# Attention turns of a hybrid encoder block: a new order of scores, transposes and weighted sums on TensorE, and transposed banks read out by two engines

## The chip, the cores and the metric

The kernel runs on one core of a Trainium2 chip. The metric is the time of one execution on the device in microseconds (us); less is better. The core has a matrix engine (TensorE, "PE" in the profile, with its weight loads shown apart as "PEld"), a vector engine (VectorE, "DVE"), a scalar engine (ScalarE, "ACT"), a general one (GpSimd, "POOL") and a queue that issues transfers (SyncE, "SP"). Each has its own queue of instructions; they wait for each other through semaphores. TensorE writes into PSUM tiles of 128 x 512 float32, called banks here, of which the kernel has eight; VectorE and ScalarE read them out.

## The reference

One layer of an encoder block over 1024 tokens of width 1024. Half of the mixed width is a convolution branch, the other half is attention with 8 heads of 64, in which each query sees an 8 x 16 neighbourhood of a grid of 16 rows by 64 columns. Cut to what the change touches:

```
s = einsum("bqhd,brqchd->bhqrc", q_r, k_win) * scale     # scores in the window
s = s + bias                                             # learned, by 2-D offset
p = softmax(s, axis=(-2, -1))
out = einsum("bhqrc,brqchd->bqhd", p, v_win)
mix = concatenate([conv_out, attn_out])
x = x + mix @ w_out
x = x + (silu(h @ w_gate) * (h @ w_up)) @ w_down         # h: RMS norm of x
```

## The kernel before

The order is written out by hand (`manual_schedule`): every engine does its instructions in the order of the Python code. Up to about 228 us come the input projections and the convolution taps, from 288 us on the output projection and the feed-forward part. Between them lies the attention loop.

The attention is cut into 32 units, numbered i. A unit is one pair of heads for a block of 128 queries. Four units in a row (a "slot", `i // 4`) share a block and so a width: `WIN` and `AR` give 253, 276, 264, 288, 341, 372, 341 and 372 keys in a window, in the order of `order`. What is outside the neighbourhood carries a bias of -1e30 from tables `tab`, which are fetched by transfers from memory. The steps of a unit:

- `score_mm(i)`: TensorE, the scores of both heads (8 matmul instructions for two units), into PSUM. Units with an odd number write into two banks of the ring `mm` (4 banks), even ones into the double bank `cv`, of which there is only one.
- `score_max(i, hh)`: VectorE adds the bias, writes the negated sum into the tile `e` and keeps its extreme in `mx`. This frees the bank.
- `score_exp(i, hh)`: ScalarE takes the exponential in place and sums it. `both` is max and exp of both heads.
- `score_norm(i)`: VectorE takes the reciprocal of the sums (`rs`), GpSimd multiplies `e` by it.
- `flip(i)`: TensorE, 12 transposes in most slots; the tile `p` lies in two `mm` banks for odd i and in `cv` for even i.
- `flip_out(i)`: reads the transposed banks back into `e`. Odd units: ScalarE, one copy for each bank. Even units: VectorE, one copy of both banks.
- `weigh(i)`: TensorE, the weighted sums of the values, 12 matmuls for three groups of keys. The value rows of a window, `vw`, come by transfers (`load_window`, `load_vw`); those of one column window (two slots) are asked for two slots ahead.
- `evac_hi`, `evac_lo`: once in four units, ScalarE and VectorE turn a finished output bank into two parts.

The loop `for i in range(4, 32, 2)` takes two units in a turn, 14 turns. In a turn TensorE does the scores of i and i + 1, the transposes of i - 3 (odd) and i - 2 (even), and the weighted sums of i - 5 and i - 4. In the turns from 14 on a job of `take_parts` (a quarter of a weight: a cast on ScalarE, a subtraction on GpSimd) is done at the end of eight turns. Behind the loop (`fill(0, 4, 5)`) come projection matmuls, the transposes of units 29, 30 and 31, and the last weighted sums.

Since even scores and even transposes share the one `cv`, its users follow each other: scores of i, two max on VectorE, transposes of i - 2, their copy, scores of i + 2.

Of the kernel before, what the change touches and what calls it, by code (L numbers as in the profile page):

```python
# [71 lines left out]
def build(ctx, tc, a):  # L72
    nc = tc.nc
    pe, act, dve, pool = nc.tensor, nc.scalar, nc.vector, nc.gpsimd
# [8 lines left out]
    def G(name, dt=F32):  # L83
        return T("G", [P, 1024], 21, name, dt)
# [10 lines left out]
    def SM(name, n=8):  # L95
        return T("sm", [P, 8], 12, name)[:, :n]

    def mm(name):
        return ps.tile([P, 512], F32, tag="mm", bufs=4, name=name)

    def tp(name):
        return ps.tile([P, 512], F32, tag="tp", bufs=2, name=name)

    def cv(name):
        return ps.tile([P, 1024], F32, tag="cv", bufs=1, name=name)
# [15 lines left out]
    def lr(w):  # L121
        return w[:, :512], w[:, 512:]
# [43 lines left out]
    def take_parts(jobs, n=4, sub=pool):  # L166
        i = pos[1]
        hi, lo = chunks[i][2]()
        w = 1024 // n
        if i == 0:  # L170
            dve.tensor_copy(hi[:, :w], raws[i][:, :w])

        def part(o):
            sl = slice(o, o + w)
            split(hi[:, sl], lo[:, sl], raws[i][:, sl], (sub,), i + o > 0)
            if o + w == 1024:
                raws.pop(i)
                issue()
        pos[1] += 1
        jobs.extend(lambda o=o: part(o) for o in range(0, 1024, w))  # L180
# [183 lines left out]
    def sum_split(h):  # L364
        if h == 0:
            cr.extend([G("crh", F32R), G("crl", F32R), ST("onesr", F32R)[:, :P]])
            dve.tensor_scalar(cr[2], ident, 0.0, 1.0, op0=OP.mult, op1=OP.add)
        split(*[w[:, h * 512:(h + 1) * 512] for w in cr[:2] + cs])
# [292 lines left out]
    def table(rh, ty):  # L661
        n = AR[rh] * NCOL[ty]
        src = tf[rh, ty].rearrange("j i h c -> (j i) (h c)")
        if rh == 0 and ty == 0:
            parts = [(G(f"tab{k}")[:, :4 * n], 4 * k) for k in range(2)]
        else:
            parts = [(H(f"tab{rh}{ty}")[:, :NH * n], 0)]
        heads = []
        for w, h0 in parts:
            nc.sync.dma_start(w, src[:, h0 * n:h0 * n + w.shape[-1]])  # L670
            heads += [w[:, o:o + n] for o in range(0, w.shape[-1], n)]
        return heads
# [10 lines left out]
    def whole(n):  # L683
        return -(-n // 32) * 32
# [29 lines left out]
    tab, et, es, pTs, os_, sums, pp, mx, cvs = {}, {}, {}, {}, {}, {}, {}, {}, {}  # L714
    at = []

    def width(s_):
        rh, cb = order[s_]
        return AR[rh] * WIN[cb][1]

    def groups(s_):
        n, m = width(s_), P if s_ == 0 else 4 * WIN[order[s_][1]][1]
        return [slice(o, min(o + m, n)) for o in range(0, n, m)]

    def score_mm(i):
        s_, hp = divmod(i, 4)
        rh, cb = order[s_]
        t = rh * 4 + cb
        c0, ncol = WIN[cb]
        s2 = cv(f"s{i}") if i > 0 and i % 2 == 0 else None  # L730
        out = []
        for hh in range(2):
            s = (mm(f"s{i}{hh}") if s2 is None else lr(s2)[hh])[:, :width(s_)]
            pe.matmul(s, qT[hh * HD:(hh + 1) * HD, hp, t * P:(t + 1) * P],  # L734
                      k4[hh * HD:(hh + 1) * HD, hp, rh * 4:rh * 4 + AR[rh], c0:c0 + ncol], start=True, stop=True)
            out.append(s)
        return out

    def score_max(i, hh, s):
        s_, hp = divmod(i, 4)  # L740
        rh, cb = order[s_]
        if i not in es:
            et[i] = G(f"e{i}").rearrange("p (h n) -> p h n", h=2)
            n, gs = width(s_), groups(s_)
            es[i] = et[i][:, :, :n]
            end = gs[-1].start + whole(gs[0].stop)
            if n < end:
                pool.memset(et[i][:, :, n:end], 0.0)
            sums[i] = SM(f"rs{i}", 2)
        mx[i, hh] = SM(f"mx{i}{hh}", 1)  # L750
        dve.tensor_tensor_reduce(out=es[i][:, hh], in0=s[hh], in1=tab[rh, cb][2 * hp + hh], scale=-1.0,  # L751
                                 scalar=3.0e38, op0=OP.add, op1=OP.min, accum_out=mx[i, hh])

    def score_exp(i, hh):
        e = es[i][:, hh]
        act.activation(e, e, AF.Exp, bias=mx.pop((i, hh)), scale=-1.0, accum_out=sums[i][:, hh:hh + 1])  # L756

    def both(i, s):
        for hh in range(2):
            score_max(i, hh, s)  # L760
            score_exp(i, hh)

    def score_norm(i):
        rs = sums.pop(i)
        dve.reciprocal(rs, rs)  # L765
        for hh in range(2):
            pool.tensor_scalar(es[i][:, hh], es[i][:, hh], rs[:, hh:hh + 1], 1.0, op0=OP.mult, op1=OP.mult)  # L767


    def flip(i):  # L770
        if i % 2 == 0:
            cvs[i] = cv(f"p{i}")
        pp[i] = lr(cvs[i]) if i % 2 == 0 else [mm(f"p{i}{r}") for r in range(2)]
        gs = groups(i // 4)
        m = whole(gs[0].stop)
        for hh in range(2):
            for g, k in enumerate(gs):
                for r, pt in enumerate(pp[i]):
                    q, o = slice(r * 64, r * 64 + 64), (hh * len(gs) + g) * 64
                    pe.transpose(pt[:m, o:o + 64], et[i][q, hh, k.start:k.start + m], ident[q, q])  # L780

    def flip_out(i, r=None):
        gs = groups(i // 4)
        m, n = whole(gs[0].stop), len(gs) * P
        w = et[i].rearrange("p h n -> p (h n)")[:m, :2 * n].rearrange("p (r n) -> p r n", r=2)
        v = w.rearrange("p r (h g q) -> p r h g q", h=2, q=64)
        pTs[i] = [v[:, :, h] for h in range(2)]
        if r is None:
            dve.tensor_copy(w, cvs[i].rearrange("p (r n) -> p r n", r=2)[:m, :, :n])
        else:  # L790
            act.copy(w[:, r], pp[i][r][:m, :n])

    def weigh(i):
        s_, hp = divmod(i, 4)
        rh, cb = order[s_]
        if hp == 0:
            os_[s_] = tp(f"o{s_}").rearrange("p (c q) -> p c q", c=4)
        gs = groups(s_)
        for g, k in enumerate(gs):
            n = whole(k.stop - k.start)  # L800
            v = vwt["first"][:, g, :] if s_ == 0 else vw[cb, rh + g]
            for hh in range(2):
                c = (2 * hp + hh) * HD
                pe.matmul(os_[s_][hh * HD:(hh + 1) * HD, hp], v[:n, c:c + HD], pTs[i][hh][:n, :, g],
                          start=g == 0, stop=g == len(gs) - 1)
# [9 lines left out]
    def evac_hi(s_):  # L815
        if not at:
            at.extend(half(f"at{h}") for h in range(2))
        act.copy(at_of(s_)[0], os_[s_])

    def evac_lo(s_):  # L820
        hi, lo = at_of(s_)
        dve.tensor_tensor(lo, os_[s_], hi.bitcast(F32), OP.subtract)
# [7 lines left out]
    def load_window(cb):  # L830
        load_vw(cb, 0, 1)
        load_vw(cb, 2, 3)
# [118 lines left out]
    def fill(m, *ks):  # L951
        if not acc:
            act.activation(warm, eps, AF.Sqrt)
        if (m, 0) not in acc:
            acc[m, 0] = mm(f"pj{m}0")
        proj(m, 0, ks, OUTER)

    for i in range(4, 32, 2):
        if i == 4:
            tab[0, 1] = tab[0, 2] = table(0, 1)  # L960
        if i == 8:
            tab[1, 1] = tab[1, 2] = table(1, 1)
        if i in (8, 12):
            load_window(i // 6)
        if i in (14, 22):
            take_parts(jobs)
        sa, sc = score_mm(i), score_mm(i + 1)
        score_max(i, 0, sa)
        score_max(i, 1, sa)
        if i > 4:  # L970
            flip(i - 3)
        score_exp(i, 0)
        score_max(i + 1, 0, sc)
        score_max(i + 1, 1, sc)
        score_norm(i - 1)
        score_exp(i, 1)
        flip_out(i - 3, 0)
        flip(i - 2)
        score_exp(i + 1, 0)
        flip_out(i - 2)  # L980
        flip_out(i - 3, 1)
        score_exp(i + 1, 1)
        score_norm(i)
        if i > 4:
            weigh(i - 5)
        weigh(i - 4)
        if i % 4 == 0 and i > 4:
            evac_hi(i // 4 - 2)
        if i % 4 == 2 and i > 6:
            evac_lo(i // 4 - 2)  # L990
        if jobs:
            jobs.pop(0)()
    fill(0, 4, 5)
    score_norm(31)
    sum_split(0)
    flip(29)
    flip_out(29, 0)
# [595 lines left out]
    for half in range(2):  # L1593
# [4 lines left out]
        w = quarter(om["u"], 0, 3)[:, part_]  # L1598
# [17 lines left out]
```

## Time and profile before

| what | us |
|---|---|
| median of 3 runs | 1014.8 (1014.24 to 1015.0) |
| the profiled execution | 1014.45 |
| its span in the trace | 1012.5 |
| the attention loop in it, first scores of i = 4 to the first projection matmul behind it | 235.16 to 288.47 |

All lines of the profile are from that one execution; their times count from the start of the span. In a line of the timeline stand: start, length, engine, line of the code, operation, written tile <- read tiles, shapes, count of merged instructions, and in brackets the idle time of the engine before it with what ended it. `PE` lengths of merged matmuls contain the modelled end of the last one.

### The profile page before, as it was taken

The page shows a single profiled execution, that of the slowest core. Times are in us where ns is not written, and L with a number is a line of the kernel's source. Part 1 is how long each engine was busy: PE and PEld are TensorE (multiplying, and loading weights), DVE is VectorE, ACT ScalarE, POOL GpSimd, SP SyncE. Part 2 cuts the span into 40 slices and gives each one's busy share as a digit, 9 for nine tenths or more (in the row PEclk, how much of TensorE's full clock was granted, in tenths as well). Part 3 has the DMA queues.
Part 4 walks back from the last instruction along what each step waited for, and adds up shares of the span by engine and source line. Part 5 has one row for each costly group of instructions (what it writes and reads, how often), then busy time and mean ns, then how long its engine had stood idle before and what let it go on. Part 6 is the DMA issues. An engine that isn't in the chain of part 4 may idle for free.

```text
span 1012.5 us, 15451 instructions
## 1 busy us (share of the span) xinstructions
PE 1004.6 (99%) x5442; PEld 843.0 (83%) x5442; DVE 781.1 (77%) x1228; ACT 476.6 (47%) x1042; POOL 457.2 (45%) x385
## 2 busy tenths in 40 slices
PE   9999999999999999999999999999999999999998
PEld 8888888886788888888888888888888888888887
DVE  5788997896779376987878778778777766768874
ACT  7556357837987255432442333333433453443432
POOL 1036674535763375275656566666565200003300
PEclk9999999999999999999999999999999999999999
DMA  9416783236514520224344343433431796634631
GB/s 349 174 50 222 204 234 94 97 104 201 177 62 165 198 98 21 67 101 166 116 147 134 125 146 126 139 132 125 155 121 59 273 373 217 209 104 142 208 118 42
DMA packets 75757, 151.72 MB, mean 150 GB/s; under 512 B 14472, under 2 KB 23560, under 8 KB 75040
## 3 DMA queue, kind: packets, MB, share of 16 engines
q1 hardware_dynamic: 73664, 147.20, 43.8%
q10 hardware_dynamic: 2016, 3.54, 1.0%
q8 instruction: 43, 0.70, 0.3%
q14 instruction: 34, 0.28, 0.1%
HBM read 112.07 MB, written 44.11 MB: 154 GB/s over the span
## 4 chain that ended last, share of the span: by engine, by line
PE 93%; DVE 3%; DMA 1%; issue 1%; POOL 1%; ACT 0%; SPq 0%; DVEq 0%; POOLq 0%
PE B L118 6%; PE B L117 6%; PE B L119 6%; PE D L117 4%; PE D L118 4%; PE D L119 4%; PE z L119 3%; PE z L117 3%; PE z L118 3%; PE pj L117 3%; PE pj L119 3%; PE gl L117 3%; PE pj L118 3%; PE gl L119 3%; PE gl L118 3%; DVE cv L381 3%
## 5 line engine op out<-in xcount | busy, mean ns | idle before, releaser
L381 DVE SCALAR_TENSOR_TENSOR cv<-u,par,cv 128x1009 f32<-128x1009 f32 (+14 forms) x92 | 117.5, 1277 | 2.3
L1559 POOL TENSOR_TENSOR ou<-ou,resm 128x512 f32<-128x512 f32 x8 | 12.8, 1615 | 137.6 <-DVE ou L1550 125.7
L408 POOL TENSOR_TENSOR pa<-pa,pr 128x1022 f32<-128x1022 f32 (+5 forms) x24 | 57.9, 2414 | 37.7 <-ACT pr L407 33.7
L109 ACT CAST op<-sr 128x512 fp32r<-128x512 f32 x77 | 47.7, 619 | 56.2 <-PE B2d L119 26.4
L113 DVE TENSOR_TENSOR op<-sr,op 128x512 fp32r<-128x512 f32 x77 | 58.2, 756 | 16.6 <-ACT op L109 16.5
L109 ACT CAST op<-wd 128x512 fp32r<-128x512 f32 x54 | 33.5, 620 | 30.7 <-DVE wd L1454 19.2
L756 ACT ACTIVATE e<-e,mx 128x341 f32<-128x341 f32 (+5 forms) x64 | 35.3, 553 | 14.7 <-DVE mx L751 14.4
L1107 DVE TENSOR_TENSOR ts<-gu,ts 128x512 f32<-128x512 f32 x36 | 40.5, 1125 | 0.6
L767 POOL TENSOR_SCALAR e<-e,rs 128x341 f32<-128x341 f32 (+5 forms) x64 | 32.7, 528 | 18.1 <-DVE rs L765 17.8
L113 DVE TENSOR_TENSOR op<-wd,op 128x512 fp32r<-128x512 f32 x54 | 39.3, 727 | 1.9 <-ACT op L109 0.8
L751 DVE CUSTOM_DVE_ANT_0 e<-s,tab 128x341 f32<-128x341 f32 (+5 forms) x64 | 27.2, 481 | 13.2 <-PE s L734 11.1
L1368 DVE TENSOR_TENSOR g<-D,g 128x512 f32<-128x512 f32 x22 | 15.2, 690 | 22.7 <-PE D L119 22.7
L435 ACT ACTIVATE sq<-z,r 128x64 f32<-128x64 f32 x96 | 28.3, 330 | 4.8 <-PE z L119 4.8
L1345 ACT ACTIVATE D<-D 128x512 f32<-128x512 f32 x22 | 12.8, 582 | 35.5 <-DVE D L1344 35.5
L407 ACT ACTIVATE pr<-u,par 128x1022 f32<-128x1022 f32 (+5 forms) x24 | 27.0, 1138 | 1.6 <-ACT vs L465 1.6
L117 PE MATMUL B2d<-op 128*128 128x512 f32 x66 | 25.7, 389 | 0.0
L118 PE MATMUL B2d<-op 128*128 128x512 f32 x66 | 25.7, 389 | 0.0
L119 PE MATMUL B2d<-op 128*128 128x512 f32 x66 | 25.7, 389 | 0.0
L1061 POOL TENSOR_TENSOR sq<-sq,sq 128x512 f32<-128x512 f32 x12 | 17.6, 1466 | 16.8 <-ACT sq L1057 16.5
L780 PEld LDWEIGHTS p<-ident,e 64*128 64x128 f32 (+1 forms) x368 | 14.7, 132 | 9.2 <-issue 4.6
L1057 ACT ACTIVATE sq<-xT 128x512 f32<-128x512 f32 x16 | 10.0, 632 | 25.4 <-DVE xT L948 25.3
L435 ACT ACTIVATION_READ_ACCUMULATOR sq<-z,r 128x1 f32 x96 | 21.7, 226 | 0.0
(1493 smaller groups left out, 3756.4 us busy)
## 6 DMA issues: line engine op xcount, KB each, us to landing
gu<-in_gu SPq DMA_DIRECT2D x44, 512.0 KB
sr<-sd SPq DMA_DIRECT2D x77, 256.0 KB
sd<-sd SPq DMA_DIRECT2D x22, 512.0 KB
wd<-in_wd SPq DMA_DIRECT2D x36, 256.0 KB
sd<-g SPq DMA_DIRECT2D x33, 256.0 KB
x<-in_x SPq DMA_DIRECT2D x8, 512.0 KB
xT<-in_xp SPq DMA_DIRECT2D x8, 512.0 KB
xd<-xT SPq DMA_DIRECT2D x16, 256.0 KB
```

The lines of the kernel that those rows point to most:

```text
L109: act.copy(hi, src)
L113: eng.tensor_tensor(*[w[..., sl] for w in (lo, src, hi.bitcast(F32))], OP.subtract)
L117: pe.matmul(acc, lh, rh, start=start, stop=False, skip_group_check=True)
L118: pe.matmul(acc, lh, rl, start=False, stop=False, skip_group_check=True)
L119: pe.matmul(acc, ll, rh, start=False, stop=stop, skip_group_check=True)
L381: dve.scalar_tensor_tensor(acc[:, o], uc[:, i], dwk[:, c, t:t + 1], acc[:, o], OP.mult, OP.add)
L408: pool.tensor_tensor(pa[:, o], pa[:, o], pr[:, o], OP.add)
L435: act.activation(sq[:, h * HD:(h + 1) * HD], z[:, h * HD:(h + 1) * HD], AF.Square, scale=r, accum_out=ss[:, h:h + 1])
L751: dve.tensor_tensor_reduce(out=es[i][:, hh], in0=s[hh], in1=tab[rh, cb][2 * hp + hh], scale=-1.0, scalar=3.0e38, op0=OP.add, op1=OP.min, a ...
L756: act.activation(e, e, AF.Exp, bias=mx.pop((i, hh)), scale=-1.0, accum_out=sums[i][:, hh:hh + 1])
L767: pool.tensor_scalar(es[i][:, hh], es[i][:, hh], rs[:, hh:hh + 1], 1.0, op0=OP.mult, op1=OP.mult)
L1107: (pool if (i, n) in ON_POOL else dve).tensor_tensor(o, l, r, OP.subtract)
```

## The change

The order within a turn becomes: scores of i + 1 (odd), transposes of i - 3 (odd), scores of i (even), weighted sums of i - 5 and i - 4, transposes of i - 2 (even). VectorE and ScalarE do max and exp of the odd unit first, then of the even one. Each `flip_out`, odd or even, is done as one copy on ScalarE and one on VectorE, a bank each. `score_norm` of the odd unit is done in the same turn and no longer in the next; that of the even unit stands at the end of the turn, behind the copies of the even transposes. The first turn does `score_norm(3)` in the place of transposes, and `score_norm(31)` behind the loop is gone, as it is in the loop now.

```
-    def flip_out(i, r=None):
+    def flip_out(i, r=None, eng=None):
...
         if r is None:
             dve.tensor_copy(w, cvs[i].rearrange("p (r n) -> p r n", r=2)[:m, :, :n])
         else:
-            act.copy(w[:, r], pp[i][r][:m, :n])
+            (eng.tensor_copy if eng else act.copy)(w[:, r], pp[i][r][:m, :n])
...
-        sa, sc = score_mm(i), score_mm(i + 1)
-        score_max(i, 0, sa)
-        score_max(i, 1, sa)
-        if i > 4:
+        sc = score_mm(i + 1)
+        if i == 4:
+            score_norm(3)
+        else:
             flip(i - 3)
-        score_exp(i, 0)
-        score_max(i + 1, 0, sc)
-        score_max(i + 1, 1, sc)
-        score_norm(i - 1)
-        score_exp(i, 1)
+        sa = score_mm(i)
         flip_out(i - 3, 0)
-        flip(i - 2)
-        score_exp(i + 1, 0)
-        flip_out(i - 2)
-        flip_out(i - 3, 1)
-        score_exp(i + 1, 1)
-        score_norm(i)
+        both(i + 1, sc)
+        both(i, sa)
+        flip_out(i - 3, 1, dve)
+        score_norm(i + 1)
         if i > 4:
             weigh(i - 5)
         weigh(i - 4)
+        flip(i - 2)
+        flip_out(i - 2, 0)
+        flip_out(i - 2, 1, dve)
+        score_norm(i)
...
     fill(0, 4, 5)
-    score_norm(31)
     sum_split(0)
```

## The prediction

> **What bounds the kernel now.** I read the page first, for the engine that is never idle, then the waits of the loop, the timeline of one steady turn, the three stretches of the loop, and the timeline just behind it. The page:
>
> ```profile
> span 1012.5 us, 15451 instructions
> PE 1004.6 (99%) x5442; PEld 843.0 (83%) x5442; DVE 781.1 (77%) x1228; ACT 476.6 (47%) x1042; POOL 457.2 (45%) x385
> ```
>
> TensorE is the bound of the whole, so the change is worth what it takes from TensorE's way through the loop, as long as what follows does not give it back. The waits between 231 and 288 us (who waited, for whom, total, times, longest):
>
> ```profile
> PEld p L780 <- issue: 4.6, 15, 1.0
> PE p L780 <- DVE mx L751: 3.0, 12, 0.5
> ...
> PEld s L734 <- DVE e L789: 0.5, 2, 0.3
> ```
>
> Nearly all that TensorE waits for in the loop is ahead of transposes (L780), on the max of VectorE (L751). For the copy of the even transposes (L789) it waits only twice, 0.5 us in all. The timeline of the turn of i = 26:
>
> ```profile
> 276.33 0.88 PEld L734 LDWEIGHTS s<-kT,qT 64*128 64x128 f32 x8 [0.17 <-issue]
> 276.33 1.42 PE L734 MATMUL s<-kT,qT 64*128 64x341 f32 x8
> ...
> 276.87 0.57 ACT L818 CAST at<-o 128x512 fp32r<-128x512 f32 x1
> 277.22 0.51 DVE L751 CUSTOM_DVE_ANT_0 e<-s,tab 128x341 f32<-128x341 f32 x1 [1.15 <-PE s L734]
> 277.30 0.68 PEld L780 LDWEIGHTS p<-ident,e 64*128 64x128 f32 x12
> 277.33 0.41 ACT L109 CAST wo06h<-wo06r 128x256 fp32r<-128x256 f32 x1
> 277.58 0.53 PE L780 MATMUL p<-ident,e 64*128 64x64 f32 x12
> ...
> 277.66 0.51 DVE L751 CUSTOM_DVE_ANT_0 e<-s,tab 128x341 f32<-128x341 f32 x1
> ...
> 278.09 0.51 DVE L751 CUSTOM_DVE_ANT_0 e<-s,tab 128x341 f32<-128x341 f32 x1
> 278.29 0.48 PEld L780 LDWEIGHTS p<-ident,e 64*128 64x128 f32 x12 [0.32 <-issue]
> ...
> 278.32 0.58 PE L780 MATMUL p<-ident,e 64*128 64x64 f32 x12 [0.21 <-DVE mx L751]
> ...
> 278.84 1.53 PE L804 MATMUL o<-e,vw 128*64 128x128 f32 x24
> ...
> 278.98 0.46 ACT L791 COPY e<-p 128x384 f32<-128x384 f32 x1
> 279.04 0.94 DVE L789 COPY e<-p 128x768 f32<-128x768 f32 x1
> ...
> 279.34 0.58 ACT L756 ACTIVATE e<-e,mx 128x341 f32<-128x341 f32 x1
> ...
> 279.96 0.67 DVE L822 TENSOR_TENSOR at<-o,at 128x512 fp32r<-128x512 f32 x1
> ...
> 280.30 0.93 PEld L734 LDWEIGHTS s<-kT,qT 64*128 64x128 f32 x8 [0.17 <-issue]
> ```
>
> By steps from start to start: scores of both units 276.33 to 277.58, 1.25. Odd transposes 0.31 (0.53 less the 0.22 of the last one, a median in the row of transposes (L780) further down). Then nothing until 278.32: 0.43, in which the even transposes stand before the shared double bank until the second max (277.66) has read it. Even transposes up to the weighted sums 0.52. Weighted sums up to the next scores 1.46. Sum 3.97, the length of the turn.
>
> **The change part by part, TensorE.** The order moves the even transposes behind the weighted sums, so that 1.46 us of other work lie over the max that they wait for. The price of each part:
>
> The wait of 0.43 goes. What could be late next is the max of the even scores: these now start about 0.62 + 0.31 = 0.93 into the turn, VectorE starts on them 0.89 later (276.33 to 277.22), the second max is let go of 0.44 + 0.63 later (277.22 to 277.66 to 278.29), 2.9 in all. TensorE arrives at 0.93 + 0.62 + 1.46 = 3.0 or later. So it just fits, with 0.1 to spare.
>
> New hand-overs. Scores to transposes costs nothing: the loads of 277.30 have no idle time before them. Weighted sums to scores costs 0.17 of idle loads (280.30). Transposes to scores, which now comes twice in a turn (odd transposes to even scores, even ones to the next odd scores), is not in the trace; I bound it by these two, 0 to 0.2 each, and take 0, since it joins the same two kinds of 64-row work as the row without a gap; but 0.1 once, as the even scores must wait for the copies (below) and their weight loads can't run ahead. Scores to weighted sums and weighted sums to transposes aren't there either; I take them at the price of the two that they replace, which is inside 0.52 and 1.46, and the bounds 0 to 0.2 on each. The page "TensorEngine Tiling (Array Packing)" of the Trainium skill, section Tiling Modes, says that changing the tiling mode drains TensorE. Counted by rows of the array the new turn has two such changes, as the old one; the trace agrees as far as the gaps at 277.30 and 280.30 go, and if transposes and scores counted as two modes, the sum would be that of the second rival.
>
> So TensorE alone needs 1.25 + 0.31 + 0.52 + 1.46 + 0.10 = 3.64 in this turn, between 3.54 and 3.94, against 3.97.
>
> **The other engines.** The copies (below, per line: ns of one, min/median/max): an odd unit's second bank goes from ScalarE to VectorE, an even unit's first bank from VectorE to ScalarE. ScalarE keeps two copies a turn; VectorE has two small ones in the place of a big one:
>
> ```profile
> L791 ACT COPY e<-p x32: 349/457/489, 237.5 to 293.7; 128x384 f32<-128x384 f32 x16, 96x384 f32<-96x384 f32 x12, 128x256 f32<-128x256 f32 x4
> ```
>
> ```profile
> L789 DVE COPY e<-p x16: 684/940/957, 233.2 to 290.5; 128x768 f32<-128x768 f32 x8, 96x768 f32<-96x768 f32 x6, 128x512 f32<-128x512 f32 x2
> ```
>
> ```profile
> L780 PE MATMUL p<-ident,e x368: 216/222/273, 232.6 to 293.0; 64*128 64x64 f32 x112, 64*96 64x64 f32 x72
> ```
>
> 512 columns take 0.68 and 768 take 0.94, so 384 take about 0.55: VectorE does 0.16 more a turn. The even copies start about 0.29 after the last transpose (278.71 to 279.00), at the start of the next turn, and end 0.55 later; with the release the even scores can start 0.9 into the turn, when TensorE comes to them (0.93). No wait, but no slack. The same page of the Trainium skill, section PSUM Bottleneck, advises to read PSUM out with both engines; by that rule alone the change would be worth the waits for L789, 0.5 us, so what I count on is the order, not the copies.
>
> VectorE and ScalarE are asked more often per us. The three stretches (to i = 14, to i = 22, to the end of the loop):
>
> ```profile
> 235.16:252.55 17.39, 15.81 (x233) 12.33 (x233) 13.39 (x56) 14.57 (x51) 8.99 (x25) 1.00 0.74 232
> 252.55:268.26 15.71, 14.79 (x226) 11.70 (x225) 12.44 (x46) 14.04 (x46) 10.68 (x25) 1.00 0.63 188
> 268.26:288.47 20.21, 19.12 (x282) 14.97 (x280) 15.88 (x58) 18.75 (x59) 15.08 (x36) 1.00 0.38 122
> ```
>
> The columns are length, then busy PE, PEld, DVE, ACT, POOL. In the last five turns ScalarE is busy for 18.75 of 20.21 us; four of them have a cast of a weight part. That is 3.75 a turn, more than TensorE's 3.64 (and 0.1 more in 372-wide turns). ScalarE's order puts exp ahead of the copy that frees the double bank, so its load becomes the pace: I take 3.84 a turn, 19.2 in all, a gain of 1.0 (bounds 0.2, if hand-overs cost 0.2, to 1.46).
>
> **Transfers.** The nine turns before that could gain 0.33 each, up to 3. But unit 16's weighted sums, in turn 20, need the value rows of the next window. Below: SP's issues of them (first and last start), one landing in the chain of work, the transfers' GB/s (last column) in two stretches, and the weighted sums of turn 20:
>
> ```profile
> L681 SPq DMA_DIRECT2D vw<-vd x9: 313/397/421, 259.6 to 263.4; - x9
> ```
>
> ```profile
> 234.33 1.64 DMA vw<-vd
> ```
>
> ```profile
> 264.00:265.00 1.00, 1.00 (x12) 0.59 (x8) 0.50 (x1) 1.00 (x4) 1.00 (x3) 1.00 0.46 129
> 265.00:266.00 1.00, 1.00 (x18) 0.63 (x14) 0.89 (x3) 0.35 (x2) 1.00 (x4) 1.00 0.22 47
> ```
>
> ```profile
> 266.80 1.53 PE L804 MATMUL o<-e,vw 96*64 96x128 f32 x24
> ```
>
> SP issues the last of them at 263.4. The chain shows 1.64 for such a landing, so 265.0 at the earliest; traffic goes on until 266 (47 GB/s in the last of these us), so 266.0 at the latest, which I take, as the queue is busy. SP does not wait for the loop there, it is behind its own tables, so the issue won't come earlier. Now the last third of unit 16's sums starts at 266.80 + 1.1 = 267.9, so nothing waits. With the new order it can't start before 266.1; then come 0.22 of sums and 0.49 of hand-over and transposes, and turn 22 starts at 266.8 at best, against 268.26: 1.45 of gain at that point, whatever the turns before saved (2.45, if the rows land at 265.0). This is the largest cut.
>
> **Behind the loop.** `score_norm(30)` now stands behind VectorE's copy of the even transposes, and `score_norm(31)` ahead of it.
>
> ```profile
> 287.46 3.33 POOL L767 TENSOR_SCALAR e<-e,rs 128x372 f32<-128x372 f32 x6 [0.69 <-DVE rs L765]
> ...
> 288.13 0.16 DVE L765 RECIPROCAL rs<-rs 128x2 f32<-128x2 f32 x1
> ...
> 288.48 0.38 PE L117 MATMUL pj<-at,wo04h 128*128 128x256 f32 x1
> ...
> 289.38 0.96 PE L780 MATMUL p<-ident,e 64*128 64x64 f32 x24
> ```
>
> Of six scalings at 0.555, the third and fourth are unit 30's, done at 289.68, just as its transposes, the second dozen from 289.38, are due (289.72, or 1.24 behind the first projection matmul). In the new order the chain is: last even transpose, 0.29, copy 0.46, reciprocal 0.26 with its release, two scalings 1.11: 2.1, against 1.4 until TensorE is there. So it stands for 0.7. Nothing else covers that; unit 31 comes later and is ready. The other moves (`score_norm(3)` early, the order of tiles) cost nothing I can name: GpSimd is busy for 34.75 of the 53.3 us, and both odd and even units are scaled a turn or more ahead of their transposes.
>
> **Sum** against the profiled execution's 1014.45, of which the span is 1012.5 (the median of the runs is 1014.8, 0.35 more, which I leave out): 1.4 at turn 22, 1.0 in the last five turns, less 0.7 behind the loop: 1.7. That gives 1012.8.
>
> **The rivals.**
> - The forecast, 0.45: a small gain, 1012.8, with its own range 1011.8 to 1014.0.
> - Hand-overs eat it, 0.20. If transposes to scores drains TensorE (0.2, twice a turn), a turn takes 3.94 and the loop gains under 0.5, which the 0.7 behind it cancels: 1014.5. For it: every change of kind but one in the trace has a gap. Against it: scores to transposes has none.
> - No late rows and no stall behind the loop, 0.23. If the value rows come in time (SP gets ahead), 0.35 a turn stay, 3 in nine turns and 1.2 in five, less 0 to 0.7: 1010.5. For it: the rows need only be 1 us earlier. Against: SP's last issue at 263.4.
> - Slower, 0.12: the double bank becomes a ring that is longer than the turn. Even scores, 0.89 to VectorE, max 0.44, 0.63 to the transposes, these 0.39, 0.29, copy 0.55, release 0.1: 3.3. VectorE does odd max and, every second turn, L822 (0.67 at 279.96) ahead, ScalarE exp (0.58) ahead of its copy. It decides when these delays pass 0.67 on the mean; at 1.0 each turn takes 4.3, 14 x 0.3 + 0.7 = 5 more: 1019.
>
> **How the numbers follow.** 0.2%, 2.0 us, is about what a measurement of this kernel can tell from no change. Of the forecast's 0.45, 0.14 lie beyond a gain of 2.0; with the third case that is faster 0.37. Same: 0.31 + 0.20. Slower: 0.12. The range leaves out the far half of the slower case and the best of the third: 1010.4 to 1015.8.
>
> **What would show it.** Right: loads of even transposes no longer idle on L751; the loop shorter by about 2.4; weighted sums (L804) of turn 20 waiting for a transfer of vw; a wait of 0.7 on L767 ahead of unit 30's transposes; ScalarE near full from turn 22 on. Wrong: gaps ahead of L734 in the middle of a turn (hand-over or copies), no wait for vw, or a loop gain that a later stage gives back.

## The result, and the profile after

The changed kernel takes 1021.09 us (median of 4 runs, 1020.61 to 1022.34) against 1014.85 for the kernel before (4 runs, 1014.24 to 1015.0): a ratio of 1.0065, 95% interval 1.0047 to 1.0082. It is 6.2 us slower, where 1012.8 was forecast and 1015.8 was the upper end. The profiled execution of the changed kernel, its first lines:

```profile
span 1019.3 us, 15467 instructions
PE 1006.5 (99%) x5442; PEld 841.8 (83%) x5442; DVE 782.4 (77%) x1242; ACT 478.3 (47%) x1042; POOL 456.9 (45%) x385
```

The span is 6.8 us longer, and the busy time of no engine moved by more than 2 us, with the same 5442 matmuls: most of what was added is waiting. The loop now lasts from 235.99 to 294.16, 58.17 us against 53.31. Its three stretches, cut at the same turns as in the prediction (to i = 14, to i = 22, to the end):

```profile
235.99:254.71 18.72, 15.51 (x234) 11.63 (x234) 13.04 (x59) 14.63 (x49) 8.02 (x22) 1.00 0.77 248
254.71:272.06 17.35, 15.15 (x231) 11.10 (x228) 12.84 (x51) 14.65 (x48) 10.79 (x25) 1.00 0.55 150
272.06:294.16 22.10, 19.70 (x288) 14.31 (x283) 16.30 (x63) 19.62 (x60) 15.38 (x36) 1.00 0.28 93
```

They are 1.33, 1.64 and 1.89 longer than before. Every turn but the first is longer, by 0.19 to 0.60: it is not one event. TensorE is idle for 2.4 us of the last stretch's 22.1 (1.1 of 20.21 before). The granted clock is 1.00 throughout, so it is no matter of the clock. The stretch behind the loop, up to the first matmul on the convolution's means, takes 5.95 against 4.76; from there to the end it is 719.2 against 719.3. So 4.86 + 1.19 = 6.05 of the 6.8 us between the two spans are found in these two places. The other 0.83 lie ahead of the loop, where the two programs are the same; the difference is there from the first 9 us on (the first matmul of L117 starts at 8.60, before at 7.73), so it is one between two executions and not a price of the change.

The waits between 231 and 296 us (who waited, for whom, total, times, longest):

```profile
DVE e L791 <- ACT e L791: 14.3, 13, 1.5
...
PEld s L734 <- DVE e L791: 8.0, 13, 1.0
PE s L734 <- DVE e L791: 6.2, 13, 0.8
PEld o L804 <- issue: 5.8, 13, 0.5
...
PE p L780 <- DVE mx L751: 1.5, 5, 0.7
```

The first line was not foreseen. Both are copies of the transposed banks, `flip_out`: VectorE's copy waits for ScalarE's, 13 times. The next two lines say who pays: the even scores wait for VectorE's copy, 13 times, 6.2 us of TensorE. What the change was to remove is indeed smaller: transposes behind the max (L751) wait 1.5 us, 3.0 before. The turn of i = 24 runs from 276.48 to 280.81. The two lines ahead of it are the even transposes of the turn before, and the copies at 276.74 and 277.32 read these:

```profile
276.05 0.45 PEld L780 LDWEIGHTS p<-ident,e 64*128 64x128 f32 x12 [0.17 <-POOL e L748]
276.06 0.59 PE L780 MATMUL p<-ident,e 64*128 64x64 f32 x12
...
276.48 0.80 PE L734 MATMUL s<-kT,qT 64*128 64x341 f32 x4
...
276.74 0.48 ACT L791 COPY e<-p 128x384 f32<-128x384 f32 x1
...
277.11 0.53 PE L780 MATMUL p<-ident,e 64*128 64x64 f32 x12
...
277.32 0.56 DVE L791 COPY e<-p 128x384 f32<-128x384 f32 x1 [1.05 <-ACT e L791]
...
277.87 0.67 DVE L822 TENSOR_TENSOR at<-o,at 128x512 fp32r<-128x512 f32 x1
...
277.93 0.84 PE L734 MATMUL s<-kT,qT 64*128 64x341 f32 x4 [0.29 <-DVE e L791]
...
278.71 1.53 PE L804 MATMUL o<-e,vw 128*64 128x128 f32 x24
...
280.41 0.59 PE L780 MATMUL p<-ident,e 64*128 64x64 f32 x12 [0.17 <-DVE mx L751]
...
280.81 0.82 PE L734 MATMUL s<-kT,qT 64*128 64x341 f32 x4
```

The even transposes are through when the odd scores start, at 276.48. ScalarE copies the first bank from 276.74 on. VectorE has nothing else to do and could copy the second bank at the same time, but stays idle for 1.05 us and starts 0.10 after ScalarE is done, at 277.32. So the chain from the last transpose to the even scores is 0.26 + 0.48 + 0.10 + 0.56 + 0.05 = 1.45 in place of the 0.9 that the prediction allowed, and TensorE, which has only 0.94 of other work (odd scores and odd transposes, 276.48 to 277.11 and 0.31 on), stands still. By starts the turn is 0.63 + 0.82 + 0.78 + 1.70 + 0.40 = 4.33.

### The profile page after: what moved, and what is told of

Read it like the earlier page. It is cut to its first block, busy times and chain, and to the rows that moved or that the text cites. A ratio compares the mean times of both kernels' runs of the same rounds, so it can differ in the third digit from the quotient of the medians.

```text
span 1019.3 us, 15467 instructions
## 1 busy us (share of the span) xinstructions
PE 1006.5 (99%) x5442; PEld 841.8 (83%) x5442; DVE 782.4 (77%) x1242; ACT 478.3 (47%) x1042; POOL 456.9 (45%) x385
## 4 chain that ended last, share of the span: by engine, by line
PE 71%; ACT 2%; DVE 1%; issue 1%; POOL 0%; DVEq 0%; POOLq 0%; ACTq 0%
PE B L117 6%; PE B L118 6%; PE B L119 6%; PE D L117 4%; PE D L118 4%; PE D L119 4%; PE pj L117 3%; PE pj L119 3%; PE pj L118 3%; ACT e L756 1%; PE B2d L118 1%; PE B2d L119 1%; PE B2d L117 1%; PE A2d L118 1%; PE A1d L118 1%; PE A0d L118 1%
## 5 line engine op out<-in xcount | busy, mean ns | idle before, releaser
L734 PE MATMUL s<-kT,qT 64*128 64x341 f32 (+5 forms) x128 | 24.3, 461 | 6.2 <-DVE e L791 6.2
L751 DVE CUSTOM_DVE_ANT_0 e<-s,tab 128x341 f32<-128x341 f32 (+5 forms) x64 | 27.7, 478 | 2.7 <-PE s L734 2.3
L791 DVE COPY e<-p 128x384 f32<-128x384 f32 (+2 forms) x28 | 15.1, 539 | 15.4 <-ACT e L791 14.3
L117 PE MATMUL B2d<-op 128*128 128x512 f32 x66 | 25.7, 389 | 0.0
L804 PEld LDWEIGHTS o<-e,vw 128*64 128x64 f32 (+1 forms) x336 | 18.1, 136 | 5.3 <-issue 5.1
```

Source lines behind the costliest of these rows:

```text
L117: pe.matmul(acc, lh, rh, start=start, stop=False, skip_group_check=True)
```

## The experiments

The suspect is in the code rather than in the chip: the two banks of an even unit are one tile, `cv`, and the program orders its two readers, one behind the other (theory A in what was expected). The rivals are the new order itself, with hand-overs on TensorE or a max that is late (theory B), and ScalarE's place in the chain, as its copy stands behind an exp (theory C). Kernels timed together share the runs of the kernel before: 1015.13 for e1 to e4, 1015.03 for the other three, 1014.85 for the change.

**One bank, one tile (e1).** The change, with the even units' double bank as two tiles of one bank each, in the loop:

```
+    def cv2(name):
+        return [wide[0].tile([P, 512], F32, tag=f"cv{r}", bufs=1, name=f"{name}{r}") for r in range(2)]
...
-        s2 = cv(f"s{i}") if i > 0 and i % 2 == 0 else None
+        s2 = cv2(f"s{i}") if i > 0 and i % 2 == 0 else None
...
-            cvs[i] = cv(f"p{i}")
+            cvs[i] = cv2(f"p{i}")
```

(The pool is opened anew around the loop for it. Units 0 and 30, ahead of the loop and behind it, where VectorE copies both banks, take two instructions in the place of one.)

> The changed kernel, but the double bank of the even units is two tiles of one bank each in the attention loop, so that VectorE's copy of the second bank no longer waits for ScalarE's copy of the first (with the double bank as one tile it does, 13 times in the changed kernel's trace). Theory A (the two copies one after the other make the ring scores, max, transposes, copies of the double bank longer than a turn, and that alone is the loss in the loop): even scores can start some 0.5 earlier in each turn; a turn of 341 columns goes from 4.34 to 3.7 to 3.8, the loop from 58.2 to 51 to 52.5 us; what stays is the wait behind the loop of about 1.2. Time 1013 to 1015. Theory B (the order itself is too long: hand-overs between kinds of matmul and the fixed order on VectorE and ScalarE): turns stay above 4.2, time 1019 to 1021.

1013.16 us (10 runs), a ratio of 0.998, 0.9971 to 0.999. Against the change that is 7.9 us from one edit that leaves every matmul, copy and place in a queue within the loop as it was. Lines 11 or 12 further down in this kernel's code are the same steps (scores L745, max L762, scaling L778, transposes L791, copies L803, sums L816). Its waits between 231 and 292 us:

```profile
PEld o L816 <- issue: 6.4, 15, 0.5
DVE e L803 <- PE p L791: 4.8, 11, 0.8
```

No copy waits for a copy any more; VectorE's waits for the transposes themselves, as it should. The end of its turn of i = 24 and, from 274.84 on, the start of the next:

```profile
274.41 0.59 PE L791 MATMUL p<-ident,e 64*128 64x64 f32 x12
...
274.78 0.31 PEld L745 LDWEIGHTS s<-kT,qT 64*128 64x128 f32 x4
...
274.84 0.79 PE L745 MATMUL s<-kT,qT 64*128 64x341 f32 x4
...
275.14 0.56 DVE L803 COPY e<-p 128x384 f32<-128x384 f32 x1 [0.27 <-PE p L791]
...
275.39 0.46 ACT L803 COPY e<-p 128x384 f32<-128x384 f32 x1
275.47 0.53 PE L791 MATMUL p<-ident,e 64*128 64x64 f32 x12
...
275.90 0.84 PE L745 MATMUL s<-kT,qT 64*128 64x341 f32 x4
```

Both engines read at once, VectorE from 275.14 and ScalarE from 275.39, and take no longer than one behind the other in the changed kernel (0.56 and 0.46, there 0.56 and 0.48). The even scores start 0.43 behind the odd transposes, not 0.82. Two side effects of the edit can be told apart from the link. Both copies still write the same tile `e`, so it was the tile that they read, not the one that they write, that held VectorE. And two tiles could let the scores of one head start as soon as their own bank is free, but here they start 0.05 behind the later of the two copies (275.39 + 0.46 = 275.85). The link between the two readers was the loss.

**The even copy whole on VectorE (e2).** The change, without its split of the even copy:

```
-        flip_out(i - 2, 0)
-        flip_out(i - 2, 1, dve)
+        flip_out(i - 2)
```

> The changed kernel, but the even units' banks are read out by VectorE in one copy, as in the kernel before; order of the turn as changed. Theory A: the chain from the last transpose to the even scores goes from 0.29 + 0.46 + 0.10 + 0.56 = 1.41 (and up to 0.3 more where ScalarE is late with its copy) to 0.29 + 0.94 = 1.23: 0.15 to 0.45 a turn less, time 1016 to 1019. Theory B: the copy's form doesn't matter, VectorE has not less to do; 1020 to 1022.

1016.73 us (10 runs), 1.0015, 1.0006 to 1.0024. A single copy has no second reader to wait for, so the link is gone here too, but 768 columns in one go are longer than two halves side by side. A turn of it:

```profile
281.59 0.84 PE L734 MATMUL s<-kT,qT 64*128 64x372 f32 x4
281.87 0.96 DVE L789 COPY e<-p 128x768 f32<-128x768 f32 x1 [0.55 <-PE p L780]
282.27 0.53 PE L780 MATMUL p<-ident,e 64*128 64x64 f32 x12
...
282.88 0.30 PEld L734 LDWEIGHTS s<-kT,qT 64*128 64x128 f32 x4 [0.21 <-DVE e L789]
```

The copy ends at 282.83, 0.25 after TensorE could be through with the odd transposes (282.27 + the prediction's 0.31 = 282.58), and the scores start 0.05 later. So between the linked halves (1021.1) and the two engines side by side (1013.2) lies the one long copy. With the even copy left as it was, the new order does not gain over the kernel before.

**The old order with the new copies (e3), and with two tiles (e5).** The kernel before, in which only the copies are changed:

```
-        flip_out(i - 2)
-        flip_out(i - 3, 1)
+        flip_out(i - 2, 0)
+        flip_out(i - 2, 1, dve)
+        flip_out(i - 3, 1, dve)
```

> The kernel before with its old order of a turn, but with the copies of the change (a bank on ScalarE, a bank on VectorE, for odd and even units). Theory A: VectorE's copy of an even unit comes after ScalarE's, which stands behind an exp: it would end at about 281.0 in the turn where the next scores now start at 280.3, so 0.7 to 0.8 a turn, 1022 to 1026: the copies alone make the loss. Theory B: the copies are harmless in the old order, 1015 to 1017.

> The old order with the copies of the change, as the third kernel, but with the even units' double bank as two tiles. Theory A (the link between the two copies is the loss): the link goes; VectorE's copy ends at 279.6 in the turn shown, ScalarE's, still behind an exp, at 280.4, against scores at 280.3: turns 0.1 to 0.2 longer than before instead of 0.8, time 1015 to 1018. Theory C (the loss is only that ScalarE's copy stands behind an exp, linked or not): stays at 1024 or more.

1027.06 us for e3 (1.0119, 1.0104 to 1.0134; a little above the expected range), 1016.87 for e5 (10 runs; 1.0019, 1.001 to 1.0028). So the copies of the change alone cost 12 us in the old order, and 10 of these are the link. The waits of the e3 loop (236 to 302 us):

```profile
DVE e L791 <- ACT e L791: 17.2, 13, 1.4
...
PE s L734 <- DVE e L791: 9.2, 13, 0.9
```

and of e5 (235 to 292 us; lines as in e1):

```profile
PEld s L745 <- ACT e L803: 5.8, 13, 0.8
...
PE s L745 <- ACT e L803: 1.9, 7, 0.5
```

The rest, 1.8 us, fits theory C: without the link the scores wait 1.9 us for ScalarE's copy, which stands behind an exp. In the new order with two tiles that wait is 0.4 us in all.

**Unit 30's scaling first (e4).** The change, and in the last turn the scaling of unit 30 ahead of the transposes and copies of unit 28:

```
+        if i == 30:
+            score_norm(i)
         flip(i - 2)
         flip_out(i - 2, 0)
         flip_out(i - 2, 1, dve)
-        score_norm(i)
+        if i < 30:
+            score_norm(i)
```

> The changed kernel, but in the last turn alone the scaling of unit 30 (reciprocal on VectorE, multiplication on GpSimd) stands ahead of the copies of the even transposes. Both theories: the loop stays at about 58 us; the wait of unit 30's transposes behind the loop on GpSimd goes, 0.7 by the prediction's estimate, up to 1.2 by the lag between the two traces. Time 1019.9 to 1020.4. If the lag behind the loop has another cause, 1021.

1020.17 us (1.005, 1.0033 to 1.0067), 0.9 below the changed kernel's 1021.09, which was timed apart from it; the intervals overlap. The stretch behind the loop shows it by itself: 5.30 in place of 5.95. The changed kernel there:

```profile
294.16 0.39 PE L117 MATMUL pj<-at,wo04h 128*128 128x256 f32 x1
...
295.07 0.59 PE L780 MATMUL p<-ident,e 64*128 64x64 f32 x12
295.38 0.16 DVE L765 RECIPROCAL rs<-rs 128x2 f32<-128x2 f32 x1
...
295.71 1.12 POOL L767 TENSOR_SCALAR e<-e,rs 128x372 f32<-128x372 f32 x2 [0.63 <-DVE rs L765]
...
296.33 0.40 PE L780 MATMUL p<-ident,e 64*128 64x64 f32 x6 [0.68 <-POOL e L767]
...
296.89 0.40 PE L780 MATMUL p<-ident,e 64*128 64x64 f32 x6 [0.15 <-POOL e L767]
```

TensorE waits 0.68 and 0.15 for the two scalings of unit 30. In e4 TensorE's idle time on them is 0.15 in all.

**Two tiles and the scaling first (e14); value rows first as well (e6).** e14 is e1 with e4's edit. e6 is e14 in which the value rows of a window (`load_window`) are asked for ahead of the large bias tables of that stage, not behind them:

```
+    load_window(3)
     tab[1, 3] = table(1, 2)
-    load_window(3)
...
+        if i in (8, 12):
+            load_window(i // 6)
         if i == 8:
             tab[1, 1] = tab[1, 2] = table(1, 1)
-        if i in (8, 12):
-            load_window(i // 6)
```

> The first kernel (two tiles) with the last turn's scaling of unit 30 ahead of the even copies. The stage from the first projection matmul behind the loop to the first mean matmul goes from 5.37 to about 4.75; time 0.6 less than 1013.16: 1012.5. If the copies in the last turn now come later than the projection can hide, 1013.2.

> As the second of this call, and the value rows of a window are asked for ahead of the bias table that now precedes them on the queue (twice). In the trace of the first kernel unit 8's sums in turn 12 wait for their rows (0.36 us) and those of turn 20 seem to (0.2): both waits go, turn 12 from 4.02 to about 3.5, time 1011.8 to 1012.2. If the table then comes late instead, turns 12 and 20 wait on VectorE's max and nothing is gained: 1012.5 or more.

e14: 1013.1 us (11 runs; 0.9983, 0.9974 to 0.9992), no different from e1; the expected 0.6 did not come. The stretch behind the loop is 5.35, and 5.37 in e1. In both, GpSimd does unit 31's two scalings first and goes straight on with unit 30's. In e1 it starts the four at 286.14, and the loads of unit 30's transposes wait for the third and the fourth of them:

```profile
286.14 2.30 POOL L778 TENSOR_SCALAR e<-e,rs 128x372 f32<-128x372 f32 x4 [0.55 <-DVE rs L776]
...
287.94 0.26 PEld L791 LDWEIGHTS p<-ident,e 64*128 64x128 f32 x6 [0.24 <-POOL e L778]
...
288.50 0.26 PEld L791 LDWEIGHTS p<-ident,e 64*128 64x128 f32 x6 [0.29 <-POOL e L778]
```

In e14 the four start at 285.57, as far ahead of the first projection matmul (0.22, and 0.21 in e1). So the queue of GpSimd, not the place of unit 30's reciprocal on VectorE, sets the time there, and the edit has nothing to win.

e6: 1018.58 us (1.0035, 1.0023 to 1.0048), 5.5 worse than e14, a miss. The rows do come earlier, but the tables come later (the last one is asked for at 261.93, in e1 by 247.5), and the turns of i = 12, 14 and 20 grow to 5.75, 5.32 and 5.28. Its waits (231 to 295 us):

```profile
ACT e L767 <- DVE mx L762: 5.6, 5, 2.8
...
DVE e L762 <- DMA tab<-tf: 2.3, 1, 2.3
```

In the turn of i = 12 the max waits 2.3 us for a table, and TensorE stands for 1.86 (to 253.66). The turn of i = 14 is long for another reason: from 256 to 259 us the granted clock is 0.50 to 0.53, and its weighted sums take 2.55 (256.67 to 259.22) in place of 1.46. In the turn of i = 20, the first to use the late table, the max starts late again; that it waits for the table there is likely, but the view does not show it. The rows behind the tables are the cheaper order of the two.

## Why the prediction was wrong

**The step that failed** is "No wait, but no slack". It let both copies start 0.29 after the last transpose and take the longer one's 0.55. That they are two halves of one tile was on the page of the code; that the second reader would be held until the first one was done was not asked. The ring had no slack, so most of the extra copy came through: 0.48 + 0.10 more in the chain showed as 0.41 more ahead of the even scores (0.82 from the odd transposes on, against 0.31 + 0.10). With two tiles the step holds (0.43).

**The rival that came true** is the last one, the ring longer than the turn. Its size came near, 4.3 us a turn and 1019 in all, against 4.33 and 1021.1; its cause was another, so the match is luck. It put the delays down to work ahead of max and copies on VectorE and ScalarE. These exist, but are small: L822 at 277.87, which comes behind the late copy, delays the max and, through it, the even transposes (0.17 of idle time at 280.41); e5 shows 1.8 us for ScalarE's exp ahead of the copy.

**The other terms of the sum** can be read in e1, which is the kernel that the prediction priced.
- TensorE's turn: 3.64 predicted, 3.75 in e1 (271.09 to 274.84): 0.63 + 0.46 + 0.77 + 1.46 + 0.43. Transposes to scores costs nothing, as taken: the loads at 274.78 have no idle time before them. Scores to weighted sums costs 0.14 (0.77 for a pair of scores that takes 0.63 when transposes follow). The prediction had a hand-over to the sums inside its 0.52 for the even transposes, which now take 0.43, so the net error there is 0.05; another 0.05 is ahead of the even scores (0.46, not 0.41), which start 0.06 behind ScalarE's copy (271.65 + 0.47, against 272.18). The rule on tiling modes that the prediction cites from the Trainium skill agrees with this if modes are counted by rows of the array: 64-row transposes and 64-row scores follow each other without a gap, 64-row scores and 128-row weighted sums do not. The rival of the hand-overs, which needed 0.2 twice a turn between transposes and scores, is ruled out.
- The last five turns: 18.99 in e1, 19.2 predicted from ScalarE's load. The stretch from i = 22 on:

```profile
267.36:286.35 18.99, 18.99 (x286) 13.98 (x282) 16.48 (x62) 18.35 (x59) 15.36 (x36) 1.00 0.44 135
```

TensorE is busy without a break and ScalarE for 18.35 of 18.99. Both are at their end, so which of them sets the pace is not shown.
- The value rows: a gain of 1.45 at turn 22 was the limit; e1 has 1.48 there (31.62 from its first turn to that of i = 22, against 33.10). But the way there is another. Of the two slow turns the one of i = 12 (4.02) shows the wait for a transfer:

```profile
251.68 0.44 PE L816 MATMUL o<-e,vw 96*64 96x128 f32 x4 [0.22 <-DMA vw<-vd]
```

In the turn of i = 20, named in the prediction, the weighted sums are 0.2 longer (265.29 to 266.95), not held for long. So the number agrees by luck: the late rows of turn 20 cost 0.2, and the turns before it won less than the prediction thought they could. In the changed kernel itself no sums wait for a transfer: it comes too late for that.
- Behind the loop: 0.7 of loss predicted for the late scaling of unit 30, 1.19 in the changed kernel, 0.6 in e1 and e14. All of it lies where the prediction put it: from the first transposes of unit 29 to the sums behind those of unit 30 it is 0.89 before, 2.15 in the changed kernel, 1.51 in e4, 1.57 in e1 and 1.56 in e14. The predicted chain (copy, reciprocal, scaling) accounts for the 0.64 that e4 wins back. The 0.6 that neither e4 nor e14 wins back is GpSimd, which does unit 31's scalings ahead of unit 30's; the prediction had named this order, but not priced it.

Without the link, then, a gain of 1.7 was a fair price (2.0 measured in e1, 1013.16 against 1015.13). The advice that the prediction cites from the Trainium skill's page "TensorEngine Tiling (Array Packing)", section PSUM Bottleneck, to read PSUM out with both engines, is borne out between e2 and e1, 3.6 us for the second engine, but in this program only where each engine has a tile of its own; with one tile it cost 4.4 us (e2 to the change).

e1 is the version to keep: 1013.16 against 1015.13 before and 1021.09 for the change.

## What to carry to other kernels

When work on one buffer is split between two engines, look at how the buffer is declared: if both halves belong to one tile, the program may order them, and the split makes the chain longer, not shorter. A row "engine A, step <- engine B, the same step" in the waits is the sign of it. And where a step is forecast with no slack, price the case in which its parts run one behind the other before giving it a small chance.

## What was not expected of the hardware

Two engines reading neighbouring banks at the same time did not slow each other (0.56 and 0.46 in e1; 0.56 and 0.48 one behind the other in the changed kernel). From 64-row scores to 128-row weighted sums TensorE loses about 0.14 us each turn, though no wait for another engine shows: in the row "PEld o <- issue" of e1 the weight loads idle for 0.43 a turn (6.4 us in 15). In e6, behind the 1.86 us for which TensorE stood (to 253.66), the granted clock was 0.50 from 256 to 258 us with TensorE busy, while in e1's loop it stayed at 1.00; that the stop brought the clock down is not tested here.
